# A third home for gathered expert rows, with the first tile's residual parked in DRAM and the score blocks placed anew

## The chip, the cores and the metric

The kernel runs on one core of a Trainium2 chip. The metric is device time in microseconds: 3100.5 us is the median of three executions before the change (3100.32, 3100.5 and 3105.6). The core has five engines, each with an instruction stream of its own that is run in order: TensorE (PE; its weight loads are listed as PEld), VectorE (DVE), ScalarE (ACT), GpSimd (POOL) and SyncE (SP), which only issues transfers. Transfers move through 16 DMA engines that all queues share.

## The reference, cut to what matters

```python
h = rms_norm(x); proj = h @ w_in                     # 512 tokens, width 2048
x = x + concat(rms_norm(attention), rms_norm(recurrent)) @ w_out
def peer_ffn(xn):                                    # 4 tiles of 128 tokens
    s1, s2 = scores of 2 x 128 keys, for 8 heads; top 16 of each, then of their sums
    e = i1 * 128 + i2                                # 128 experts per token, of 16384
    g = softmax(top)
    act = gelu(einsum('chkd,cd->chk', u_tab[e], xn))
    return einsum('chk,chkd->cd', g * act, v_tab[e])
x = x + peer_ffn(rms_norm(x))
```

## The kernel before

The attention and recurrent half fills about the first 640 us. After it, `acc` [128 x 4 x 2048] holds the residual of the four token tiles; it is also what the expert half adds to and what is written out. The normalised activations stand transposed in `FH` and `FL` (a high and a low part; every product is three matmuls, `mm3`).

**Two ways through the experts.** Tiles 1 to 3 (384 tokens) go through all 16384 experts as dense matmuls: 128 score blocks ("S": 128 experts x 384 tokens, 2 half blocks of 24 matmuls each), gelu, times a gate matrix, and then the value matmuls ("V"). Tile 0 is done by gathering: 128 rows of `u_tab` and then 128 of `v_tab`, 1 MB each (one row of 2048 floats for each of 128 tokens). `gather` issues one such transfer on GpSimd's queue; `side` is one side step: VectorE takes row j, forms a dot product with `xg` (j < 128) or adds it, weighted, into `acc[:, 0, :]` (j >= 128), and then calls `gather` for a later row. At j = 127 ScalarE's gelu and a product make the weights W0 from the dots.

**Weights stream.** `need` hands out the next half block in a fixed order and, first, issues the loads that come after (`emit_next`): a raw load of 512 KB on SP's queue, ScalarE's copy `hi` (L130), VectorE's remainder `lo` (L131). Four slots of hi and lo exist, so up to four half blocks are converted or being converted.

**The gate stage** (from about 965 us). `NB4` = 96 gate groups of four tokens build the gate matrix. For each, VectorE makes five one-hot products (`onehots`, L847, L848, L850; three buffers, two groups ahead), TensorE 12 small matmuls (L863), and ScalarE copies the result into the staging buffer `stg` (L865). There is one `stg`; it holds eight groups, then ScalarE's queue stores it to `GD` in DRAM (L868, 2 MB). Between the groups stand `park` calls: a score block whose gelu result is saved to DRAM (`AD`). 44 blocks are parked, ten before this stage, 32 in the loop (one for every third group) and two behind it. Side steps stand at groups 3, 9, ..., 39 and at every third group from 45: 24 in all, with one buffer for rows (`rowp`). In this part the order of the instructions on each engine is made by a scheduler from the program's order and its own estimate of when operands are ready.

**The main stage** (from about 1351 us) is written out in order by hand (`manual_schedule`). PSUM is divided anew (`ps_s`: two buffers pS; `ps_v`: six pV). The loop runs over `JOBS`: the S blocks 44 to 127, mixed with V jobs, then the V jobs of the parked blocks. `gates` loads a slice of GD on SP's queue. After each half unit `pace` adds 0.585 (0.43 for the parked part) to a debt, and each whole unit of it is one side step; rows have a second buffer in pool `ep`. What a job leaves behind (`fin`: gelu and gating, or the eviction of pV into `acc`, L996) is run in the next job. After the loop come the last evictions, the store of tiles 1 to 3, and any side steps that are left.

Of the kernel before, what the change touches and what calls it, by code (L numbers as in the profile page):

```python
# [7 lines left out]
F32 = mybir.dt.float32  # L8
# [8 lines left out]
DRAM = bass.MemoryType.DRAM  # L17

S, D = 512, 2048
# [18 lines left out]
def body(tc, nc, d, dbg=None):  # L38
    v, s, g, pe, sy = nc.vector, nc.scalar, nc.gpsimd, nc.tensor, nc.sync
# [3 lines left out]
    def pool(name, bufs=1, **kw):  # L43
        cm = tc.tile_pool(name=name, bufs=bufs, **kw)
        p = cm.__enter__()
        stk.append((p, cm))
        return p

    def close(p):
        i = [q is p for q, _ in stk].index(True)  # L50
        cm = stk.pop(i)[1]
        cm.__exit__(None, None, None)
# [4 lines left out]
    acc = accp.tile([128, NTT, D], F32, name="acc")  # L57
# [46 lines left out]
    pools = [base]  # L104
# [335 lines left out]
    for hb in range(2):  # L440
# [34 lines left out]
        for u in range(3):  # L475
            hi, lo = need("wuq", hb, u)
            for m in range(2):
# [5 lines left out]
                i = 2 * u + m  # L483
# [5 lines left out]
                else:  # L489
                    t_ = ap.tile([128, S], F32, name="qrx", bufs=3)  # L490
                    v.tensor_scalar(t_, ps, col(C_QHR), None, op0=OP.mult)
                    j = 2 * (i - 4)
# [115 lines left out]
    xg = xgp.tile([128, D], F32, name="xg")  # L608
# [23 lines left out]
    for k in range(KT):  # L632
        ps = bank()
        for t in range(NTT):
# [3 lines left out]
        v.scalar_tensor_tensor(XL[:, :, k, :], pv, col(C_FG + k), XH[:, :, k, :].bitcast(F32),  # L638
                               op0=OP.mult, op1=OP.subtract)
    v.tensor_tensor(xg, xns[0], grow, op=OP.mult)  # L640
    close(fp)
    egp = pool("eg", side="right")

# [3 lines left out]


    NCH = TD // 32
    dr = pool("dr", space=DRAM)  # L650
    GD = dr.tile([NCH, NBLK // GRP, 128, GRP * 32], F32, name="GD")
    AD = dr.tile([PARK, 128, TD], F32, name="AD")
    pkp = pool("park")
# [11 lines left out]
    def park():  # L665

        b = parked[0]
        if b >= PARK:
            return
        parked[0] += 1  # L670
        ps = bank()
        s_matmuls(b, ps[:, :TD])
        a = pkp.tile([128, TD], F32, name="pact", bufs=2)
        s.activation(a, ps[:, :TD], AF.Gelu)  # L674
        s.dma_start(AD[b], a)
# [123 lines left out]

    rowp = pool("rowp")  # L800
    rows, ng = {}, [0, 0]

    def gather(*pools):
        j = ng[0]
        if j >= 256:
            return
        ng[0] += 1
        r = pools[j % len(pools)].tile([128, D], F32, name="row", bufs=1)
        g.indirect_dma_start(out=r, out_offset=None, in_=d["un" if j < 128 else "vn"],  # L809
                             in_offset=bass.IndirectOffsetOnAxis(ap=E0[:, j % 128:j % 128 + 1], axis=0))  # L810
        rows[j] = r

    def side(*pools):

        j = ng[1]
        if j >= 256:
            return
        ng[1] += 1
        r = rows.pop(j)
        if j < 128:  # L820
            v.scalar_tensor_tensor(r, r, 1.0, xg, op0=OP.mult, op1=OP.mult, accum_out=dots[:, j:j + 1])  # L821
            if j == 127:
                s.activation(W0, dots, AF.Gelu)
                v.tensor_tensor(W0, W0, G0, op=OP.mult)
        else:
            v.scalar_tensor_tensor(acc[:, 0, :], r, W0[:, j - 128:j - 127], acc[:, 0, :], op0=OP.mult, op1=OP.add)  # L826
            if j == 255:
                g.dma_start(d["out"][0:128, :], acc[:, 0, :])
        gather(*pools)

    gp = pool("gate")
    iox = gp.tile([128, 64, 2], BF, name="iox")
    v.tensor_copy(iox, cst[:, K_IOTA:K_IOTA + 128].rearrange("p (a b) -> p a b", b=2))
    gather(rowp)
    NT = 4
    NB4 = TD // NT
    oh = {}

    def onehots(q):

        o2 = gp.tile([128, NT, 64, 2], BF, name="o2", bufs=3)
        o1 = gp.tile([128, NT, 64, 2], BF, name="o1", bufs=1)
        o3 = gp.tile([128, 3, NT, 64, 2], BF, name="o3", bufs=3)
        c = slice(NT * q, NT * q + NT)
        sh = [128, NT, 64, 2]
        io = iox[:, None].to_broadcast(sh)
        v.tensor_tensor(o2, io, e2T[:, c, None].to_broadcast(sh), op=OP.is_equal)  # L847
        v.tensor_tensor(o1, io, e1T[:, c, None].to_broadcast(sh), op=OP.is_equal)  # L848
        for j in range(3):
            v.tensor_tensor(o3[:, j], o1, g3T[:, j, c, None].to_broadcast(sh), op=OP.mult)  # L850
        oh[q] = (o2.rearrange("p t a b -> p t (a b)"), o3.rearrange("p j t a b -> p j t (a b)"))
# [3 lines left out]
    def gate_mm(q):  # L855

        o2, o1 = oh.pop(q)
        if q % 8 == 0:
            stg[0] = gp.tile([128, 128, 32], F32, name="stg", bufs=1)
        ps = bank()  # L860
        for i in range(4):
            for j in range(3):
                pe.matmul(ps[:, i * 128:(i + 1) * 128], o2[:, i], o1[:, j, i], start=j == 0, stop=j == 2)  # L863
        qq = q % 8
        s.activation(stg[0][:, :, qq * 4:(qq + 1) * 4].rearrange("p a t -> p t a"),  # L865
                     ps.rearrange("p (t a) -> p t a", t=4), AF.Copy)
        if qq == 7:
            s.dma_start(GD[q // 8].rearrange("g p x -> p g x"), stg[0].rearrange("p (g a) t -> p g (a t)", a=GRP))  # L868
# [1 line left out]
    for q in range(2):  # L870
        onehots(q)
    for q in range(NB4):
        if q % 3 == 0:
            park()
            if q % 6 == 3 or q > 42:
                side(rowp)
        if q + 2 < NB4:
            onehots(q + 2)
        gate_mm(q)
# [9 lines left out]
    ep = pool("ep")  # L889
# [31 lines left out]
    def pace(x):  # L921
        debt[0] += x
        while debt[0] >= 1:
            debt[0] -= 1
            side(rowp, ep)

    gather(rowp, ep)
    post = []
    def fetch(b):
        if b < PARK:  # L930
# [6 lines left out]
    for ji in range(PARK, len(JOBS)):  # L937
        job = JOBS[ji]
        if job[0] == "S":
# [4 lines left out]
            for hf in range(2):  # L944
                hi, lo = need("ud", b, hf)
                for k in range(8):
                    kk = hf * 8 + k
                    mm3(ps, hi[:, k * 128:(k + 1) * 128], lo[:, k * 128:(k + 1) * 128],
                        XH[:, 1:, kk, :], XL[:, 1:, kk, :], kk == 0, kk == KT - 1)
                if ji == PARK and hf == 0:  # L950
                    gates(b // GRP)
                for f in post:
                    f()
                post = []
                pace(RATE)
# [6 lines left out]
        else:  # L962
# [13 lines left out]
            for pr in range(2):  # L976
                hi, lo = need("vd", gi, dc, pr)
                for t in range(3):
                    for bj in range(2):
                        ph, pl = Pt[gi * GRP + 2 * pr + bj]  # L980
                        cs = slice(bj * 512, (bj + 1) * 512)
                        pe.matmul(pss[t], ph[:, t, :], hi[:, cs], start=pr + bj == 0, stop=False)  # L982
                        pe.matmul(pss[t], ph[:, t, :], lo[:, cs], start=False, stop=False)  # L983
                        pe.matmul(pss[t], pl[:, t, :], hi[:, cs], start=False, stop=pr + bj == 2)  # L984
                for f in post:
                    f()
                post = []
                if tail and pr == 1:
                    b = gn * GRP + dc
                    gated(At.pop(b), b)  # L990
                pace(0.43 if tail else RATE)
# [9 lines left out]
    for f in post:  # L1001
        f()
    while ng[1] < 256:
        side(rowp, ep)
    ctx.__exit__(None, None, None)
    while stk:
        close(stk[-1][0])
# [77 lines left out]
```

## Time and profile before

| | |
|---|---|
| median of three executions | 3100.5 us |
| profiled execution: own time, span of its instructions | 3107.04 us, 3104.9 us |
| PE busy | 3043.2 us, 98% |
| DVE, ACT, POOL busy | 74%, 35%, 13% |
| bytes moved | 691.13 MB, mean 223 GB/s |
| mean granted TensorE clock | 0.986 of full speed |
| main stage, 1360 to 3080 us | PE 1720.00 us busy, DMA engines 80% |

Times in the rows are from the start of the span. A row in brackets tells how long the engine stood idle before the instruction and what ended it. An engine name with a q (SPq) is its queue issuing a transfer.

### The profile page before, as it was taken

To read this page: it belongs to the slowest core of one execution; us is meant where nothing else is said; L and a number is where in the kernel's file an instruction comes from. 1 tells how busy PE (TensorE), PEld (TensorE's weight loads), DVE (VectorE), ACT (ScalarE), POOL (GpSimd) and SP (SyncE) were. 2 spreads that over 40 slices of the span, in tenths; PEclk is the share of its full clock that TensorE was granted. 3 is DMA by queue.
4 is the path that set the end of the run, shared out by engine and by line. 5 is a ranking of instruction groups with operands and counts; after the bars stand their busy time and mean duration, and the time that the engine had idled before them with its cause. 6 is when DMAs were issued, how large, how long until landed. Compare 5 with 4: busy or idle time off the path is not lost.

```text
span 3104.9 us, 39324 instructions
## 1 busy us (share of the span) xinstructions
PE 3043.2 (98%) x15443; PEld 2630.8 (85%) x15443; DVE 2284.7 (74%) x3456; ACT 1096.5 (35%) x1371; POOL 393.9 (13%) x280
## 2 busy tenths in 40 slices
PE   8999999999999999999999999999999999999999
PEld 7777565678899998999999999999999999888887
DVE  4465544448999888757777777777777777788887
ACT  4455332342234444443333333333333333333332
POOL 0000000000000011001212112122211212211111
PEclk9999898999999999999999999999999999999999
DMA  7222211232245887678787787877878778878876
GB/s 247 87 78 75 88 55 41 88 108 83 89 129 195 269 274 255 200 264 290 278 296 284 283 301 274 299 284 281 296 281 296 285 282 292 298 277 295 290 283 234
DMA packets 247306, 691.13 MB, mean 223 GB/s; under 512 B 17040, under 2 KB 128272, under 8 KB 213456
## 3 DMA queue, kind: packets, MB, share of 16 engines
q1 hardware_dynamic: 152832, 382.15, 36.8%
q0 software_dynamic: 37008, 269.50, 23.2%
q10 hardware_dynamic: 57280, 36.97, 3.9%
q8 instruction: 121, 1.98, 0.3%
q14 instruction: 65, 0.53, 0.0%
HBM read 650.40 MB, written 38.14 MB: 222 GB/s over the span
## 4 chain that ended last, share of the span: by engine, by line
PE 57%; issue 0%; DVE 0%; ACT 0%
PE pV L984 11%; PE pV L983 11%; PE pV L982 11%; PE pS L161 8%; PE pS L163 8%; PE pS L162 8%; PE ps L161 0%; PE ps L162 0%; PE ps L163 0%; PE ps L863 0%; DVE acc L996 0%; ACT pact L674 0%; DVE o L850 0%; ACT hi L130 0%
## 5 line engine op out<-in xcount | busy, mean ns | idle before, releaser
L130 ACT ACTIVATE hi<-raw 128x1024 fp32r<-128x1024 f32 x631 | 667.8, 1061 | 1489.4 <-PE pS L162 487.6
L131 DVE TENSOR_TENSOR lo<-raw,hi 128x1024 fp32r<-128x1024 f32 x631 | 771.1, 1222 | 495.2 <-ACT hi L130 481.6
L161 PE MATMUL pS<-FH,hi 128*128 128x384 f32 x1344 | 449.9, 335 | 1.3 <-ACT pact L674 1.3
L163 PE MATMUL pS<-FH,lo 128*128 128x384 f32 x1344 | 450.0, 335 | 0.0
L162 PE MATMUL pS<-FL,hi 128*128 128x384 f32 x1344 | 449.5, 334 | 0.0
L984 PE MATMUL pV<-hi,FL 128*128 128x512 f32 x960 | 374.7, 390 | 0.0
L983 PE MATMUL pV<-lo,FH 128*128 128x512 f32 x960 | 374.7, 390 | 0.0
L982 PE MATMUL pV<-hi,FH 128*128 128x512 f32 x960 | 373.4, 389 | 0.0
L161 PE MATMUL ps<-FH,hi 128*128 128x384 f32 (+1 forms) x960 | 342.8, 357 | 0.3 <-ACT hi L130 0.3
L809 POOL DMA_INDIRECT row<-in_un,E x128 | 175.6, 1372 | 1319.3 <-DVE row L821 819.3
L163 PE MATMUL ps<-FH,lo 128*128 128x384 f32 (+1 forms) x960 | 337.8, 352 | 0.6 <-DVE lo L131 0.6
L162 PE MATMUL ps<-FL,hi 128*128 128x384 f32 (+1 forms) x960 | 338.1, 352 | 0.0
L821 DVE SCALAR_TENSOR_TENSOR row<-row,xg 128x2048 f32<-128x2048 f32 x128 | 292.5, 2285 | 22.0 <-DMA row<-in_un,E 22.0
L826 DVE SCALAR_TENSOR_TENSOR acc<-row,W,acc 128x2048 f32<-128x2048 f32 x128 | 300.2, 2345 | 0.0
L809 POOL DMA_INDIRECT row<-in_vn,E x128 | 192.4, 1503 | 804.8 <-DVE acc L826 754.0
L161 PEld LDWEIGHTS pS<-FH,hi 128*128 128x128 f32 x1344 | 252.3, 188 | 4.7 <-ACT pact L674 1.7
L162 PEld LDWEIGHTS pS<-FL,hi 128*128 128x128 f32 x1344 | 252.3, 188 | 3.1
L163 PEld LDWEIGHTS pS<-FH,lo 128*128 128x128 f32 x1344 | 252.2, 188 | 0.0
L996 DVE TENSOR_TENSOR acc<-pV,acc 128x512 f32<-128x512 f32 x384 | 240.9, 682 | 8.3 <-PE pV L984 8.3
L984 PE MATMUL pV<-hi,pl 128*128 128x512 f32 x576 | 224.4, 390 | 0.0
L983 PE MATMUL pV<-lo,ph 128*128 128x512 f32 x576 | 224.2, 389 | 0.0
L982 PE MATMUL pV<-hi,ph 128*128 128x512 f32 x576 | 224.0, 389 | 0.0
(281 smaller groups left out, 4423.2 us busy)
## 6 DMA issues: line engine op xcount, KB each, us to landing
raw<-in_ud SPq DMA_DIRECT2D x256, 512.0 KB
raw<-in_vd SPq DMA_DIRECT2D x256, 512.0 KB
G<-GD SPq DMA_DIRECT2D x33, 768.0 KB
GD<-stg ACTq DMA_DIRECT2D x12, 2048.0 KB
raw<-in_win SPq DMA_DIRECT2D x44, 512.0 KB
raw<-in_wo SPq DMA_DIRECT2D x32, 512.0 KB
raw<-in_wq SPq DMA_DIRECT2D x32, 512.0 KB
AD<-pact ACTq DMA_DIRECT2D x44, 192.0 KB
```

The costliest lines, as they stand in the source:

```text
L130: s.activation(hi, raw, AF.Copy)
L131: v.tensor_tensor(lo, raw, hi.bitcast(F32), op=OP.subtract)
L161: pe.matmul(out, ah, bh, start=start, stop=False)
L162: pe.matmul(out, ah, bl, start=False, stop=False)
L163: pe.matmul(out, al, bh, start=False, stop=stop)
L809: g.indirect_dma_start(out=r, out_offset=None, in_=d["un" if j < 128 else "vn"], in_offset=bass.IndirectOffsetOnAxis(ap=E0[:, j % 128:j % ...
L821: v.scalar_tensor_tensor(r, r, 1.0, xg, op0=OP.mult, op1=OP.mult, accum_out=dots[:, j:j + 1])
L826: v.scalar_tensor_tensor(acc[:, 0, :], r, W0[:, j - 128:j - 127], acc[:, 0, :], op0=OP.mult, op1=OP.add)
L982: pe.matmul(pss[t], ph[:, t, :], hi[:, cs], start=pr + bj == 0, stop=False)
L983: pe.matmul(pss[t], ph[:, t, :], lo[:, cs], start=False, stop=False)
L984: pe.matmul(pss[t], pl[:, t, :], hi[:, cs], start=False, stop=pr + bj == 2)
L996: v.tensor_tensor(a, pss[t], a, op=OP.add)
```

## The change

Tile 0's residual, `acc[:, 0, :]`, is stored to a DRAM buffer `RD` before the gate stage, on SP's queue. From then until side step 127 this part of `acc` is a home for gathered rows; after step 127 GpSimd's queue loads the residual back, and from there `xg`, whose last reader was step 127, is a home instead. A table, `row_buf`, says where row j goes: two homes in the gate stage (the first 19 rows), three in the main stage. `side` now issues gathers until it is `ahead` of the steps by two, or three in the main stage; the first 19 gathers belong to the gate stage.

Blocks stand at groups 0, 3 and 6 of every eight groups, until 44 are parked; side steps stand at group 0 of every eight and at group 11 of every sixteen: 18 in all. `RATE` and the other paces are as before.

```diff
+    dr = pool("dr", space=DRAM)
+    RD = dr.tile([128, D], F32, name="RD")
+    sy.dma_start(RD, acc[:, 0, :])
     close(fp)
...
+    NG0 = 19
+    late = {}
+    def row_buf(j):
+        if j < NG0:
+            i = j % 2
+        else:
+            i = (j - NG0 + NG0 % 2) % 3
+        if i == 0:
+            return rowp.tile([128, D], F32, name="row", bufs=1)
+        if i == 1:
+            return acc[:, 0, :] if j < 128 else xg
+        return late["ep"].tile([128, D], F32, name="row", bufs=1)
-    def gather(*pools):
+    def gather():
...
-        r = pools[j % len(pools)].tile([128, D], F32, name="row", bufs=1)
+        r = row_buf(j)
...
                 v.tensor_tensor(W0, W0, G0, op=OP.mult)
+                g.dma_start(acc[:, 0, :], RD)
...
-        gather(*pools)
+        if j + ahead[0] >= NG0 and "ep" not in late:
+            return
+        while ng[0] < min(256, ng[1] + ahead[0]):
+            gather()
+    ahead = [2]
...
-    gather(rowp)
+    gather()
+    gather()
...
-        if q % 3 == 0:
+        if q % 8 in (0, 3, 6):
             park()
-            if q % 6 == 3 or q > 42:
-                side(rowp)
+        if q % 8 == 0 or q % 16 == 11:
+            side()
...
-            side(rowp, ep)
-    gather(rowp, ep)
+            side()
+    late["ep"] = ep
+    ahead[0] = 3
+    while ng[0] < ng[1] + 3:
+        gather()
...
     while ng[1] < 256:
-        side(rowp, ep)
+        side()
```

## Rows read from the trace of the kernel before

**Rows 1.** The page: TensorE's busy time, share of the span and instructions.
```profile
PE 3043.2 (98%) x15443; PEld 2630.8 (85%) x15443; DVE 2284.7 (74%) x3456; ACT 1096.5 (35%) x1371; POOL 393.9 (13%) x280
```

**Rows 2.** Windows: length, busy PE, PEld, DVE, ACT, POOL; clock, DMA share, GB/s.
```profile
970.64:987.23 16.59, 12.30 (x85) 11.41 (x85) 14.35 (x28) 5.42 (x6) 1.89 (x2) 0.90 0.61 214
987.23:1255.51 268.28, 249.84 (x1934) 244.05 (x1933) 222.35 (x436) 122.56 (x138) 27.48 (x22) 0.96 0.80 265
...
1160.42:1170.83 10.41, 10.41 (x86) 10.25 (x85) 9.49 (x19) 5.56 (x6) 1.68 (x1) 1.00 0.75 257
1255.51:1328.36 72.85, 72.85 (x590) 71.75 (x589) 49.14 (x112) 35.70 (x41) 0.00 (x0) 1.00 0.57 174
1328.36:1350.85 22.49, 19.36 (x134) 18.66 (x133) 9.00 (x11) 11.12 (x14) 1.08 (x1) 1.00 0.75 219
1360.00:3080.00 1720.00, 1720.00 (x8503) 1540.41 (x8502) 1364.84 (x1382) 538.57 (x630) 336.15 (x230) 1.00 0.80 287
```

**Rows 3.** Timeline of ScalarE, end of the gate stage and first blocks after it.
```profile
1334.51 0.38 ACTq L868 DMA_DIRECT2D GD<-stg  x1
...
1345.20 1.06 ACT L130 ACTIVATE hi<-raw 128x1024 fp32r<-128x1024 f32 x1 [2.72 <-PE ps L162]
1349.36 1.06 ACT L130 ACTIVATE hi<-raw 128x1024 fp32r<-128x1024 f32 x1 [3.10 <-PE ps L162]
...
1359.97 1.06 ACT L130 ACTIVATE hi<-raw 128x1024 fp32r<-128x1024 f32 x1 [3.76 <-DMA raw<-in_ud]
```

**Rows 4.** Waits, 970 to 1351 us: waiter and releaser, total, times, longest.
```profile
ACT stg L865 <- DMA GD<-stg: 61.7, 11, 11.0
DVE lo L131 <- ACT hi L130: 38.4, 12, 7.1
...
DVE row L821 <- DMA row<-in_un,E: 19.9, 13, 3.8
PE ps L863 <- ACT stg L865: 12.3, 3, 5.3
PE ps L863 <- DVE o L850: 11.4, 4, 4.3
```

**Rows 5.** Timeline of ScalarE around two stores of stg (groups 31 and 39).
```profile
1093.25 0.38 ACTq L868 DMA_DIRECT2D GD<-stg  x1
...
1104.12 1.14 ACT L865 ACTIVATE stg<-ps 128x512 f32<-128x512 f32 x1 [2.83 <-DMA GD<-stg]
...
1123.62 0.38 ACTq L868 DMA_DIRECT2D GD<-stg  x1
...
1139.43 2.10 ACT L865 ACTIVATE stg<-ps 128x512 f32<-128x512 f32 x2 [10.97 <-DMA GD<-stg]
```

**Rows 6.** Tiles row and out: transfers from issue to landing, us.
```profile
DMA to landing us min/median/max: 5.4/7.3/10.7
...
DMA to landing us min/median/max: 4.4/4.4/4.4
```

**Rows 7.** Timelines of VectorE and GpSimd, the last 23 us.
```profile
3082.82 2.35 DVE L826 SCALAR_TENSOR_TENSOR acc<-row,W,acc 128x2048 f32<-128x2048 f32 x1
...
3099.82 0.69 DVE L996 TENSOR_TENSOR acc<-pV,acc 128x512 f32<-128x512 f32 x1 [0.67 <-PE pV L984]
...
3085.46 0.58 POOL L828 DMA_DIRECT2D out<-acc  x1 [9.13 <-DVE acc L826]
```

**Rows 8.** Timeline of VectorE in the gate stage; line 821, 970 to 1351 us.
```profile
1133.29 1.22 DVE L131 TENSOR_TENSOR lo<-raw,hi 128x1024 fp32r<-128x1024 f32 x1
...
1136.10 0.42 DVE L848 TENSOR_TENSOR o<-iox,e1T 128x512 bf16<-128x512 bf16 x1
...
1136.77 1.09 DVE L850 TENSOR_TENSOR o<-o,g3T 128x512 bf16<-128x512 bf16 x3
...
L821 DVE SCALAR_TENSOR_TENSOR row<-row,xg x24: 2279/2291/2293, 973.0 to 1234.4; 128x2048 f32<-128x2048 f32 x24
```

**Rows 9.** Timeline of SP's queue after the gate stage's last store.
```profile
1346.40 0.38 SPq L895 DMA_DIRECT2D G<-GD  x1
```

More of the change, by code (lines that the diff above doesn't have):

```diff
@@ L649, in body @@
     NCH = TD // 32
-    dr = pool("dr", space=DRAM)
     GD = dr.tile([NCH, NBLK // GRP, 128, GRP * 32], F32, name="GD")
@@ L811, in gather, with side @@
         rows[j] = r
-    def side(*pools):
+    def side():
         j = ng[1]
```

## The prediction, made before the kernel ran

> **What bounds the kernel now.** I read the page first: TensorE is busy 98% of the span [rows 1], so only TensorE's lost time, or work behind its last matmul, can move the end. Then I cut the span into windows at the starts of gate groups [rows 2]. From 1360 to 3080 us TensorE is busy for all 1720.00 us at full clock: nothing that VectorE, the gathers or the loads do there costs time now, and nothing can be won there. The loss to look at is in the gate stage.
>
> A clean period of that stage, one score block and three gate groups, takes 10.41 us (third window of [rows 2]). A half block takes 4.16 us, read from the two ScalarE splits that start as its slots come free, at 1345.20 and 1349.36 [rows 3]; a block is so 8.32 us and a gate group (10.41 - 8.32) / 3 = 0.70 us. Against that price the windows lose:
> - start, 970.64 to 987.23: 16.59 - 10.41 = 6.2 us, at a clock of 0.90;
> - middle, 987.23 to 1255.51, 23 periods: 268.28 - 23 x 10.41 = 28.9 us, at 0.96;
> - 1255.51 to 1328.36, 7 periods: 72.85 - 72.87 = 0;
> - end, 1328.36 to 1350.85, three gate groups and the two blocks that trail the loop: 22.49 - 2.1 - 16.6 = 3.8 us.
> That is 38.9 us. The views of waits say whom TensorE waited for: gate matmuls for the copies into stg (12.3 us) and for one-hots (11.4 us) [rows 4]; the rest is matmuls at the lower of the two clock levels (1.2 of 2.4 GHz) after such a gap. Behind both stands the single stg: ScalarE waits 61.7 us, 11 times, for the store of the previous 32 columns, and while it stands its splits stand too, so VectorE's lo waits for hi (38.4 us) and one-hots queue behind it [rows 4]. A store takes 10.9 us when a block follows it soon (issued 1093.25, next copy 1104.12) and 15.8 us at its longest (1123.62 to 1139.43) [rows 5]. The last seven periods have the same kind of waits, but no side step, and lose nothing: it takes stg's wait and VectorE's side steps together.
>
> **The change part by part.** *Saving RD.* One 1 MB store on SP's queue before the stage, whose source is long ready. It lies under projections; a direct 1 MB transfer landed after 4.4 us [rows 6]. I take 0, with 4.4 as upper bound if the loads queued behind it were late.
>
> *Homes of rows.* Two in the stage, three afterwards. VectorE waited 19.9 us for rows in the stage [rows 4], which can go. After 1360 us TensorE has no gap to give back: 0. Side steps are 2.35 us each [rows 7]; there are still 256.
>
> *Side steps in the stage: 18 instead of 24.* The order on the engines is the scheduler's, and it runs them as early as it can, about one in every period: all 24 of them start between 973.0 and 1234.4 us, though the program has the last at group 93 [rows 8]. This is why the 7 periods have none. VectorE's own work in a period is 3 x 1.69 us of one-hots (0.67 from the start of an o1 to that of the three o3, an o2 between, and 1.02 for these) and two lo of 1.22 us [rows 8], 7.5 of 10.41 us. One side step fits, and a third more now that two rows can wait. So I expect 18 steps packed into the first half, at the density of before or above.
>
> *Blocks at groups 0, 3 and 6 of eight.* Each reuse of stg now has a block, 8.32 us, between the store and the copy that waits for it. With a store of 10.9 us ScalarE's wait falls to 2 to 4 us, with 15.8 to at most 8. I take the middle loss from 28.9 to 8 us: two or three us at each of the first three or four reuses, where side steps are dense, nothing later, as in the quiet window. Bounds: 0 (as that window) and 20 (two thirds of today's, if side steps decide). The start I leave at 6.2, since the first step still waits for its row ahead of a one-hot; bounds 5 and 10.
>
> *The end of the stage.* Blocks come 3 to every 8 groups, so the 34 that are left are used up at group 88: seven gate groups and then the switch of PSUM pools have no block beside them. Call t the end of that last block. The store of groups 80 to 87 is issued two copies after group 87, about 6.2 us before t (8.3 for the block, less 2.1), and lands after 10.9 us, at t + 4.7; then eight copies of 1.05 us [rows 5] follow, done at t + 13.1. One-hots cannot be sooner than t + 10: five groups wait for a buffer and take 1.69 us each. The last store is issued at t + 13. Before, it was issued at 1334.51 and 1346.40 is when SP could go on to the gate load that waits for it, 11.9 us [rows 3, 9]; the two trailing blocks covered that. SP's queue holds the raw loads for block 46 on behind that gate load. From 1346.40 to the split of raw half 46:1, which waited for its load, was 13.6 us (1359.97) [rows 3, 9], and right behind that split (1.06) on ScalarE stands the first gelu of pS (0.5); block 46 needs the PSUM buffer that it frees. So block 46 can start 11.9 + 15.2 = 27 us after the last store's issue, at t + 40. Without any loss it would start at t + 5.6 (eight gate groups) + 16.6 (blocks 44 and 45) = t + 22.2. The loss is 18 us, and some 2 us of lower clock behind the gap: 20 us, against 3.8 now, so +16. Bounds: +5 (if a hit at the raw loads is smaller because only 46:0 matters and the burst lands in half the time) and +21 (a store of 15.8 us there).
>
> *The tail.* I counted the paced steps: 424 half units with 0.585 or 0.43 each make 234. Before, 24 + 234 is more than 256 and the last step ran at 3082.82, 17 us ahead of the last eviction (3099.82) [rows 7]. Now 18 + 234 = 252: four steps follow the last eviction, in the written order. From the end of that eviction: step 252, 2.35 us; it frees the home of row 255, whose gather lands 5.4 to 10.7 us after its issue [rows 6], about 6 with little else moving: 2.35 + 0.25 + 6 = 8.6, later than steps 253 and 254 (7.05); step 255 ends at 11.0; the store of out is issued 0.3 us later (3085.17 to 3085.46 [rows 7]) and lands in 4.4. Before, the final store took the same 4.4 us from the same eviction. So +11 us, bounds 10 (5.4) and 16 (10.7). The Trainium skill (DMA: Bandwidth & Descriptors, Anatomy of one DMA) gives 2.0 us plus bytes over 436 GB/s for a transfer issued from GpSimd, an estimated 4.4 us for this 1 MB row; by it the tail would be +9.4 instead of +11. The rows show no gather under 5.4 us, so the measured value stands.
>
> *Restoring RD.* The load is issued by GpSimd behind side step 127, and step 128 now comes one half unit (4.15 us) later. It will stand some 4 us for the landing, and lo and evictions behind it. TensorE has two split half units in hand, 8.3 us: 0, bound +4.
>
> **Sum.** Start 0, middle -20.9, end +16, tail +11, RD 0: +6 us. The profiled execution took 3107.04 us for a span of 3104.9, above the median of 3100.5; the difference is set on the median: 3106.5 us. A change of 0.2%, 6.2 us, is about what these runs can tell from none.
>
> **The rivals.** *A, the forecast* (+6, own range -3 to +14), 0.45; of it 0.29 inside 0.2% and 0.16 above.
>
> *B, side steps fill VectorE and the middle stalls stay.* For it: all the loss lies where side steps are, and they stay at least as dense. Against: the first reuses that follow a block at once have short stores. Middle 20 instead of 8: +18, 3118.5 us. It decides if more than half of the first five reuses still hold a gate matmul over 3 us. 0.20, slower.
>
> *C, the end is covered.* If the last store lands while blocks 44 and 45 still run and raw half 46:1 is in time, the end costs +5 and not +16; with the middle at 3 the sum is -25.9 + 5 + 11 = -10, 3090.5 us. For it: slots held four halves before, 16.6 us of work. Against: the load came 13.6 us after SP was free. It decides if block 46 starts within 3 us of block 45's end. The Trainium skill (Trainium Kernel Development and Optimization, Best Practices) advises double buffering, and by that rule the second home alone should pay; the rows give it 11.4 us of one-hot waits at most, -11.4 without the end and the tail. 0.22: 0.19 faster, 0.03 the same.
>
> *D, the middle has less to give outside the profile.* The profiled run is 6.5 us longer than the median; if these are stg stalls, the middle gives 14.4 and the sum is +12.5, 3113 us. Nothing in the rows speaks against it. 0.13, slower.
>
> Together: faster 0.19, within 0.2% 0.32, slower 0.49. Range: C's 3090.5 at the low end, B's 3118.5 with two us of the tail's bound at the high end: 3090 to 3120.
>
> **What would show it.** The stage's window in the new trace: gate matmuls waiting after group 48 should be gone, but a gap before the gate groups 91 to 95, before the first pS and before block 46, with SP's gate load late. After the last pV eviction four side steps, the last of them waiting for its row. I am wrong if block 46 is not late, if the middle keeps its gaps, or if steps 252 to 255 run ahead of the last eviction.

## The result, and the profile after

The changed kernel takes 3137.74 us (median of four, 3136.38 to 3142.51) against 3103.05 us of the kernel before beside it (median of four, 3100.32 to 3113.49): ratio 1.0108, 95% interval 1.0081 to 1.0135. It is slower by about 35 us, outside the predicted range, whose upper end was 3120. The profiled execution has a span of 3134.5 us against 3104.9, and these 29.6 us are what the traces can place.

The page of the changed kernel first: TensorE's busy time is the same to 0.4 us [rows 1], so what was added is time in which it stood idle.

```profile
PE 3043.6 (97%) x15443; PEld 2630.3 (84%) x15443; DVE 2284.6 (73%) x3456; ACT 1096.4 (35%) x1371; POOL 397.0 (13%) x281
```

The windows of the changed kernel, cut as in [rows 2] at gate groups: groups 0 to 2 with a block, groups 3 to 23, groups 24 to 87, groups 88 to the first block of the main stage, from there to block 46, and from there to the last matmul's end.

```profile
966.74:988.27 21.53, 14.65 (x86) 13.07 (x85) 18.48 (x32) 5.66 (x6) 2.81 (x3) 0.76 0.81 284
988.27:1098.32 110.05, 85.57 (x637) 82.48 (x637) 85.01 (x153) 39.69 (x45) 16.93 (x14) 0.91 0.73 254
1098.32:1342.75 244.43, 244.43 (x1922) 240.66 (x1921) 169.18 (x369) 121.60 (x136) 0.00 (x0) 1.00 0.64 198
1342.75:1355.67 12.92, 8.64 (x97) 6.68 (x96) 9.55 (x25) 9.15 (x10) 0.00 (x0) 0.81 0.21 61
1355.67:1379.14 23.47, 19.35 (x97) 19.03 (x97) 3.84 (x4) 2.50 (x3) 1.87 (x2) 0.86 0.92 292
1379.14:3114.07 1734.93, 1734.93 (x8544) 1551.57 (x8544) 1379.73 (x1401) 538.10 (x630) 342.07 (x234) 1.00 0.81 288
```

With the prediction's prices, 8.32 us a block and 0.70 us a group, the first window loses 11.1 us; the second, 21 groups and 8 blocks, 110.05 - 81.3 = 28.8; the third, 64 groups and 24 blocks, 244.43 - 244.5 = 0; the fourth, 8 groups, 7.3; the fifth, two blocks, 6.8. The last window is 2.7 us longer than in the kernel before (1732.2 by the same cut): from 1379.14 to 1395.70 us the mean granted clock was 0.83, behind the start of block 46 in the kernel before 1.00, and 0.17 of 16.6 us is an estimated 2.8 us. The difference of the spans:

| part | before | after | difference | predicted |
|---|---|---|---|---|
| begin of the first gate group | 970.6 | 966.7 | -3.9 | 0 |
| start (groups 0 to 2) | 6.2 | 11.1 | +4.9 | 0 |
| middle (groups 3 to 87) | 28.5 | 28.7 | +0.2 | -20.9 |
| end, up to block 46 and behind it (7.3 + 6.8 + 2.7) | 3.8 | 16.8 | +13.0 | +16 |
| start of the last matmul to end of span | 5.5 | 20.8 | +15.3 | +11 |
| sum | | | +29.5 | +6 |

(Before, the middle lost 28.9 in the prediction's windows, which ended at group 72 and then lost nothing; cut at group 88 it is 28.5.)

The waits of the changed kernel between 966 and 1356 us. They answer to [rows 4]:

```profile
ACT stg L887 <- DMA GD<-stg: 71.8, 11, 15.3
DVE lo L131 <- ACT hi L130: 57.9, 18, 11.6
...
PE ps L885 <- DVE o L872: 33.3, 10, 12.1
...
DVE row L837 <- DMA row<-in_un,E: 4.5, 4, 1.4
```

The second home did what it was for: VectorE's wait for rows in `row` fell from 19.9 to 4.5 us. But ScalarE's wait for stg rose from 61.7 to 71.8 us, although each copy that reuses stg now has a block ahead of it. The stores themselves are longer. ScalarE's timeline at the first store and at the fifth:

```profile
1002.35 0.38 ACTq L890 DMA_DIRECT2D GD<-stg  x1
...
1025.47 2.73 ACT L887 ACTIVATE stg<-ps 128x512 f32<-128x512 f32 x3 [15.28 <-DMA GD<-stg]
...
1153.21 0.40 ACTq L890 DMA_DIRECT2D GD<-stg  x1
...
1165.10 3.01 ACT L887 ACTIVATE stg<-ps 128x512 f32<-128x512 f32 x3 [4.04 <-DMA GD<-stg]
```

From issue to the next copy the first store takes 23.1 us and the fifth 11.9; before it was 10.9 to 15.8 [rows 5]. The second took 22.5, the third 18.1, the fourth 14.3; the fifth to the tenth take 11.5 to 12.6 and the eleventh 8.8.

What else used the 16 DMA engines meanwhile is in the view of the queues (packets, MB, share of the 16 engines): q0 carries GpSimd's gathers, q10 ScalarE's stores, q1 SP's loads. First store (1002.35 to 1025.47 us), fifth (1153.21 to 1165.10) and last (1355.65 to 1364.46):

```profile
q0 software_dynamic: 576, 4.19, 46.5%
q10 hardware_dynamic: 4398, 2.49, 34.6%
q1 hardware_dynamic: 483, 1.72, 18.2%
...
q10 hardware_dynamic: 4317, 2.37, 64.7%
q1 hardware_dynamic: 311, 1.14, 35.6%
...
q10 hardware_dynamic: 4112, 2.10, 84.9%
```

In the first two of these windows q10 also carries the results of parked blocks, 0.3 to 0.4 MB. The store's queue has 34.6% of 23.1 us, 64.7% of 11.9 and 84.9% of 8.8, which is 8.0, 7.7 and 7.5 us, so the store's own work is nearly the same in all three. The rest of the first store's time went to gathers (10.8 us) and raw loads (4.2 us), and the packets of the three queues together fill 99% of the engines' time. No more than two gathers are in flight at once, but 4.19 MB is four of them: side steps go on while the store is under way, and each frees a home for the next gather. The fourth store has no gather beside it any more, but 2.1 MB of raw loads. And the two stores of [rows 5] were not alone either; q0 in their windows (1093.25 to 1104.12 and 1123.62 to 1139.43 us of the kernel before):

```profile
q0 software_dynamic: 95, 0.65, 17.7%
...
q0 software_dynamic: 286, 2.09, 40.0%
```

Line 837, the side step, shows what goes on meanwhile (counts, min/median/max ns, first and last start):

```profile
L837 DVE SCALAR_TENSOR_TENSOR acc<-acc,xg x9: 2277/2283/2293, 959.1 to 1093.8; 128x2048 f32<-128x2048 f32 x9
...
L837 DVE SCALAR_TENSOR_TENSOR row<-row,xg x9: 2282/2286/2293, 973.1 to 1087.0; 128x2048 f32<-128x2048 f32 x9
```

The 18 steps, spread over 96 groups in the program, run between 959.1 and 1093.8 us, one per 7.9 us (before: 24 in 261 us, one per 11 [rows 8]), and with them their gathers. How a long store reaches TensorE is seen on VectorE's timeline ahead of the gap of 11.8 us in front of group 13 (gaps are given from the start of one matmul to the start of the next):

```profile
1029.09 1.23 DVE L131 TENSOR_TENSOR lo<-raw,hi 128x1024 fp32r<-128x1024 f32 x1 [8.30 <-ACT hi L130]
...
1030.57 2.29 DVE L837 SCALAR_TENSOR_TENSOR row<-row,xg 128x2048 f32<-128x2048 f32 x1
...
1032.78 1.14 DVE L872 TENSOR_TENSOR o<-o,g3T 128x512 bf16<-128x512 bf16 x3
```

VectorE stands 8.30 us at a lo whose hi is behind ScalarE's standing copy, then does the lo and a side step that the order has put ahead, and only then the one-hots for which TensorE waits.

The end of the stage came as predicted. ScalarE's timeline, then SP's queue [rows 3, 9]:

```profile
1355.65 0.38 ACTq L890 DMA_DIRECT2D GD<-stg  x1
...
1377.65 1.06 ACT L130 ACTIVATE hi<-raw 128x1024 fp32r<-128x1024 f32 x1 [5.38 <-DMA raw<-in_ud]
1378.61 0.47 ACT L984 ACTIVATE pact<-pS 128x384 f32<-128x384 f32 x1
```

```profile
1364.46 0.38 SPq L917 DMA_DIRECT2D G<-GD  x1
```

The last store is issued at 1355.65 and landed after 8.7 us with nothing beside it (11.9 was taken); the gate load, free from then, is followed by the raw loads; the second of them lets its split begin 13.2 us later (13.6 was taken), and block 46 starts behind the gelu, at 1379.14.

The tail, VectorE and then GpSimd [rows 7], and the transfer's time from the list of issues:

```profile
3114.11 0.69 DVE L1021 TENSOR_TENSOR acc<-pV,acc 128x512 f32<-128x512 f32 x1 [0.67 <-PE pV L1009]
...
3124.91 2.35 DVE L843 SCALAR_TENSOR_TENSOR acc<-row,W,acc 128x2048 f32<-128x2048 f32 x1 [3.08 <-DMA row<-in_vn,E]
```

```profile
3117.33 2.93 POOL L825 DMA_INDIRECT row<-in_vn,E  x1 [7.22 <-DVE acc L843]
3127.56 0.58 POOL L845 DMA_DIRECT2D out<-acc  x1 [7.31 <-DVE acc L843]
```

```profile
out<-acc POOLq DMA_DIRECT2D x1, 1024.0 KB, 4.2
```

Four steps follow the last eviction, from 3114.72 us on; the last waits for row 255, 7.6 us after its gather began (6 was taken), and the span ends 6.9 us after the store's issue (4.4 was taken).

### The profile page after: what moved, and what is told of

It is laid out like the page before. It is cut to its first block, busy times and chain, and to the rows that moved or that the text cites. A ratio compares the mean times of both kernels' runs of the same rounds, so it can differ in the third digit from the quotient of the medians.

```text
span 3134.5 us, 39313 instructions
## 1 busy us (share of the span) xinstructions
PE 3043.6 (97%) x15443; PEld 2630.3 (84%) x15443; DVE 2284.6 (73%) x3456; ACT 1096.4 (35%) x1371; POOL 397.0 (13%) x281
## 4 chain that ended last, share of the span: by engine, by line
PE 90%; DVE 5%; DMA 2%; ACT 1%; issue 1%; SPq 0%; POOL 0%; POOLq 0%; ACTq 0%; DVEq 0%
PE pV L1008 11%; PE pV L1009 11%; PE pV L1007 11%; PE ps L161 7%; PE ps L163 7%; PE ps L162 7%; PE pS L161 7%; PE pS L163 7%; PE pS L162 7%; PE ps L388 2%; PE ps L389 2%; PE ps L387 2%; DMA GD<-stg 2%; PE ps L885 2%; PE ps L546 1%
## 5 line engine op out<-in xcount | busy, mean ns | idle before, releaser
L1009 PEld LDWEIGHTS pV<-hi,FL 128*128 128x128 f32 x960 | 180.1, 188 | 37.8
L1007 PEld LDWEIGHTS pV<-hi,FH 128*128 128x128 f32 x960 | 180.2, 188 | 35.3
L1008 PEld LDWEIGHTS pV<-lo,FH 128*128 128x128 f32 x960 | 180.2, 188 | 35.4
L825 POOL DMA_INDIRECT row<-in_un,E x82 | 111.6, 1362 | 753.4 <-DVE row L837 477.7
## 6 DMA issues: line engine op xcount, KB each, us to landing
GD<-stg ACTq DMA_DIRECT2D x12, 2048.0 KB, 11.9
```

## The experiments

Two theories of the middle at first. T (transfers): the gathers stretch stg's store. V (VectorE): the packed side steps fill VectorE. For each kernel the loss of the middle is that of groups 3 to 87, with the prices above; the number of blocks in it differs, so the working is given. All kernels below but the two without steps were executed once. The kernel with another pace, whose gate stage is that of the changed kernel, loses 28.5 us in the middle (354.21 - 325.7) where that one loses 28.7.

**Small gathers.**

```diff
+    row0 = rowp.tile([128, D], F32, name="row0")
+    v.memset(row0, 0.0)
...
         if i == 0:
+            return row0
...
+        n = 16 if j < NG0 else 128
-        g.indirect_dma_start(out=r, ...
-                             in_offset=...(ap=E0[:, j % 128:j % 128 + 1], axis=0))
+        g.indirect_dma_start(out=r[:n], ...
+                             in_offset=...(ap=E0[:n, j % 128:j % 128 + 1], axis=0))
```

> The first 19 gathers move 16 partitions of a row tile instead of 128 (128 KB instead of 1 MB each; the other partitions hold old data, so the output differs); the side steps on VectorE are as in the changed kernel, and as dense or denser. Theory T (transfers): two homes let gathers bunch, and these stretch the store of stg from 11 us (as after group 40 in the changed kernel) to 23, 22, 18 and 14 us; ScalarE, then lo, then one-hots stand for it. T expects the first four stores at 10 to 13 us and the gaps of 11.8 and 12.3 us at groups 12 and 20 gone (under 2 us), the span about 25 us under the changed kernel's 3134.5. Theory V (VectorE): the packed side steps fill VectorE and delay the one-hots; V expects the gaps to stay (8 us or more each) although the stores are short.

Measured: span 3115.1. The middle's window:

```profile
992.75:1324.10 331.35, 328.28 (x2557) 322.07 (x2557) 254.25 (x521) 162.57 (x181) 15.93 (x14) 0.99 0.64 194
```

85 groups and 32 blocks are 325.7 us, so it loses 5.6 us instead of 28.7; the largest gap is 2.3 us. The span fell by 19 us and not by 25. The first store, in ScalarE's timeline:

```profile
1006.79 0.38 ACTq L895 DMA_DIRECT2D GD<-stg  x1
1018.95 3.03 ACT L892 ACTIVATE stg<-ps 128x512 f32<-128x512 f32 x3 [4.27 <-DMA GD<-stg]
```

12.2 us instead of 23.1. The 18 steps were as dense, 963 to 1076 us. T holds, V alone does not.

**Quick steps.**

```diff
+            w = 512 if j < 18 else D
-            v.scalar_tensor_tensor(r, r, 1.0, xg, ...
+            v.scalar_tensor_tensor(r[:, :w], r[:, :w], 1.0, xg[:, :w], ...
```

> The first 18 side steps work on 512 of the 2048 columns of a row (the dots of these rows are partial, so the output differs), about 0.7 us instead of 2.3 us of VectorE each; gathers are whole. T expects stores of 18 us and more again and at least one gap over 8 us between groups 8 and 24. V expects gaps under 3 us and the stage about 25 us shorter, whatever the stores take.

Measured: span 3125.6; the first two stores as long as in the changed kernel (23.1 and 22.3 us on ScalarE's timeline; the first):

```profile
1002.66 0.41 ACTq L891 DMA_DIRECT2D GD<-stg  x1
1025.78 2.73 ACT L888 ACTIVATE stg<-ps 128x512 f32<-128x512 f32 x3 [15.26 <-DMA GD<-stg]
```

The middle, 988.74 to 1332.94 us, loses 18.5 us (344.2 - 325.7). After the first store TensorE has two gaps close together, of 4.1 and 6.0 us; after the second only 1.6 and 1.7. T's wording (a gap of over 8 us) fails by its letter, V's (under 3) too. Shorter steps give back 10 of 28.7 us: VectorE's load decides in part what a long store costs.

**One home.**

```diff
-            i = j % 2
+            i = 0
-    ahead = [2]
+    ahead = [1]
-    gather()
     gather()
```

> One home for rows in the gate stage (one gather in flight), all else as in the changed kernel: 18 side steps, blocks at groups 0, 3 and 6 of eight, four steps left for the tail. T expects stores of 11 to 16 us as before the change, no gap over 4 us after group 8, and the middle of the stage at a loss of 3 to 10 us instead of 29: a span of about 3112 us. A rival, that the new place of the blocks itself does the harm, expects the gaps of 11 to 12 us to stay, 3130 us or more. V, whose steps are now one a period again, expects 5 to 12 us less.

Measured: span 3141.2. T was wrong here: the middle loses 31.0 us (356.78 - 325.7), with gaps of 2.6 to 4.1 us at each of the first five reuses. The middle's window, then the first store on ScalarE's timeline:

```profile
991.31:1348.09 356.78, 338.73 (x2558) 331.39 (x2557) 259.64 (x522) 160.69 (x181) 17.43 (x16) 0.96 0.70 221
...
1005.21 0.42 ACTq L889 DMA_DIRECT2D GD<-stg  x1
1021.83 2.77 ACT L886 ACTIVATE stg<-ps 128x512 f32<-128x512 f32 x3 [8.74 <-DMA GD<-stg]
```

With one gather in flight at a time the store still takes 16.6 us, later ones without steps 11.6 to 13.0. Two homes make the loss come in two large pieces, one home in five; the sum is nearly the same. What this left open, whether the gather or the blocks' new place does it, the last two kernels settle.

**Blocks at their old place.**

```diff
-        if q % 8 in (0, 3, 6):
+        if q % 3 == 0:
             park()
```

> Blocks at every third group again, so that two blocks trail the loop; two homes, 18 side steps and the tail as in the changed kernel. T expects stores of 18 us and more in the first third of the stage and at least as much loss in the middle as now (29 to 45 us); the end of the stage, from the last gate group to the start of block 46, back to a loss of some 4 us from 17. If the place of the blocks is the cause, the middle falls to 25 us or less.

Measured: span 3133.5. The middle loses 40.3 us (332.74 less 85 groups and 28 blocks, 292.5), ScalarE waits up to 15.4 us for a store; the end loses 2.3 us and block 46 starts 16.8 us after the first block, as before the change. So the new place takes 12 us off the middle when gathers are dense, and gives 14 back at the end (7.3 + 6.8 against 2.3 and 0.1, and 2.7 behind it).

**The pace.**

```diff
-    RATE = 0.585
+    RATE = 0.605
```

> The changed kernel with the pace 0.605 instead of 0.585, so that 18 + 241 paced steps are more than 256 and none is left behind the last eviction. If the four left steps make the tail, the time from the last matmul to the end falls from 20.8 us to the 5.5 us of the kernel before, and the span from 3134.5 to about 3119; nothing else moves. Rival: VectorE's extra steps or the store of out on GpSimd's queue still stretch the tail; then it stays above 10 us.

Measured: span 3117.5, tail 6.3 us, main stage from block 46 on 1734.4 us, TensorE busy throughout. VectorE's last instruction is again an eviction, and no step stands behind it:

```profile
3111.66 0.69 DVE L1021 TENSOR_TENSOR acc<-pV,acc 128x512 f32<-128x512 f32 x1 [0.67 <-PE pV L1009]
```

The tail of 20.8 us falls to 6.3, so the four steps left over are 14.5 of the 15.3 us by which the tail had grown, and the main stage has room for them.

**Two blocks behind the loop.**

```diff
-        if q % 8 in (0, 3, 6):
+        if q % 8 in (0, 3, 6) and parked[0] < PARK - 2:
```

> The changed kernel with the last two blocks taken out of the loop, so that they trail it as before the change. If the missing cover makes the loss at the end, block 46 starts 16.6 us after the first block of the main stage (23.5 now), and the last eight groups lose under 4 us; the loop's last third has fewer blocks to cover groups, which may cost a few us there. Span about 3122. Rival: the loss comes from something else at the switch, and block 46 stays late by 5 us or more.

Measured: span 3131.0. Windows of groups 3 to 87, 88 to the main stage, and blocks 44 and 45:

```profile
986.23:1329.02 342.79, 315.57 (x2461) 308.11 (x2461) 246.37 (x507) 157.48 (x177) 16.09 (x14) 0.96 0.68 217
1329.02:1361.62 32.60, 30.02 (x192) 25.80 (x192) 16.80 (x40) 12.42 (x14) 0.94 (x1) 0.79 0.69 202
1361.62:1378.37 16.75, 16.75 (x97) 16.75 (x97) 9.55 (x9) 4.09 (x5) 0.94 (x1) 1.00 0.93 329
```

Block 46 is on time (16.75 us), so the missing cover was its cause. But with the two blocks taken from the loop twelve groups stand bare instead of seven: the middle loses 33.7 (342.79 - 309.1 for 30 blocks) and the last eight groups with the two blocks 10.4 us. The expectation of 4 us, and of 3122 for the span, was wrong: cover was moved, not made.

**The kernel before without steps in the stage.**

```diff
-            if q % 6 == 3 or q > 42:
-                side(rowp)
-    RATE = 0.585
+    RATE = 0.66
```

> The kernel before, with no side step in the gate stage and the pace 0.66 instead of 0.585, so that all 256 are in the main stage. Theory T and V both: no gathers and no steps there, so the middle of the stage loses under 4 us instead of 28.5, and the main stage, where TensorE has no gap now, takes 24 more steps (56 us of VectorE in 1750) for nothing: a span of 3070 to 3078 us against 3104.9, ratio 0.990. Rival: the main stage's VectorE and DMA are nearer to full than the rows show, and the steps that come there cost as much as they cost in the stage: ratio 0.997 or more.

Measured: 3072.29 us (median of four) against 3108.32 of the kernel before beside it (seven), ratio 0.988, interval 0.9863 to 0.9896; span 3071.0. It beats both kernels. Windows: groups 3 to 87, 88 to the main stage, block 46 to the last matmul:

```profile
980.58:1276.55 295.97, 293.57 (x2366) 288.01 (x2365) 213.25 (x476) 150.22 (x169) 0.00 (x0) 1.00 0.62 190
1276.55:1316.91 40.36, 39.02 (x291) 38.38 (x288) 20.10 (x38) 19.30 (x23) 0.94 (x1) 1.00 0.73 229
...
1333.66:3065.80 1732.14, 1732.14 (x8545) 1548.87 (x8544) 1422.20 (x1437) 538.00 (x628) 386.63 (x254) 1.00 0.83 300
```

The start loses 0.7 us (11.08 - 10.4), the middle 3.5 (with 28 blocks), the end 1.5; the main stage takes the 24 steps with TensorE busy all the time, VectorE at 82% and the DMA engines at 83%.

**The changed kernel without steps in the stage.**

```diff
-        if j < NG0:
-            i = j % 2
-        else:
-            i = (j - NG0 + NG0 % 2) % 3
+        i = j % 3
-    NG0 = 19
+    NG0 = 2
-        if q % 8 in (0, 3, 6):
+        if q % 8 in (0, 3, 6) and parked[0] < PARK - 2:
             park()
-        if q % 8 == 0 or q % 16 == 11:
-            side()
-    RATE = 0.585
+    RATE = 0.66
```

> The changed kernel with no side step in the gate stage, the pace 0.66, three homes in the main stage from the first row on, and two blocks behind the loop. If homes and the blocks' place are worth nothing where there is no gap, it equals the kernel before without steps, within 0.2%. If the blocks around the reuse of stg or the third home help, it is faster than that one by 5 us or more.

Measured: 3080.44 us, ratio to the kernel before 0.9911 (0.9894 to 0.9927), span 3077.0: slower than the last one, not equal. Groups 88 to the main stage:

```profile
1289.28:1322.19 32.91, 30.25 (x193) 26.10 (x193) 16.80 (x40) 12.42 (x14) 0.94 (x1) 0.79 0.67 195
```

The middle, with 30 blocks, loses 3.4 us (312.55 - 309.1), as without the new place; the end 10.7, its bare groups. The third home changes nothing in a main stage that has no gap (1731.8 us from block 46 to the last matmul's start in both).

**Small stores.**

```diff
+    for c in range(NCH):
+        g.dma_start(GD[c].rearrange(...), d["un"][c * 256:(c + 1) * 256].rearrange(...))
...
-            s.dma_start(GD[q // 8].rearrange(...), stg[0].rearrange(...))
+            s.dma_start(GD[q // 8, :, :16].rearrange(...), stg[0][:16].rearrange(...))
```

> The changed kernel, homes, steps, blocks and whole gathers as they are, but each store of stg moves 16 of the 128 partitions (the rest of the gate buffer in DRAM is filled with other data by DRAM-to-DRAM copies before the gate stage, so the output differs and the stretch before the stage may be some us longer). If the way from gathers to the gaps leads through stg's store and ScalarE's wait for it, ScalarE waits under 1 us per reuse, and the middle of the stage loses under 6 us instead of 28.7 although gathers and steps are as dense. If gathers or steps hurt in another way (late raw loads, VectorE full), 15 us or more stay.

Measured: the stage begins 21 us later, so the span, 3128.1, says little; the middle loses 6.9 us (332.64 - 325.7). ScalarE's wait for stores, 960 to 1350 us:

```profile
ACT stg L889 <- DMA GD<-stg: 1.8, 2, 1.0
```

Gathers whole, steps as dense (980 to 1094 us), store short: some 22 of 28.7 us are gone, though the loss is not quite under the 6 us expected. The way from gathers to TensorE leads through stg's store. The rest, 6.9 us here and 5.6 with small gathers, is what packed steps cost without a long store.

**One home, small gathers.** The edits of the third and the first experiment together.

> One home in the stage as before (18 steps, one gather in flight), with gathers of 16 partitions (other rows of data, output differs). With whole gathers the stores took 16.6 us and the middle lost 31.0 us. If a single gather in flight already stretches the store, the first stores take 11 to 12 us here and the middle loses under 6 us. If the blocks' place or the steps cause that loss, 15 us or more stay.

Measured: span 3104.9. The middle's window and the first store on ScalarE's timeline:

```profile
986.21:1312.98 326.77, 326.41 (x2557) 320.83 (x2556) 258.92 (x522) 162.63 (x181) 17.89 (x16) 1.00 0.65 195
```

```profile
1000.12 0.41 ACTq L894 DMA_DIRECT2D GD<-stg  x1
1012.75 3.04 ACT L891 ACTIVATE stg<-ps 128x512 f32<-128x512 f32 x3 [4.76 <-DMA GD<-stg]
```

The loss is 1.0 us instead of 31.0, the store 12.6 us instead of 16.6. So whole gathers, one at a time, were the cause; the blocks' place was not, and neither were the steps, which come one per 10.3 us here.

## Why the prediction was wrong

**The step that failed** is "Blocks at groups 0, 3 and 6 of eight": "With a store of 10.9 us ScalarE's wait falls to 2 to 4 us, with 15.8 to at most 8. I take the middle loss from 28.9 to 8 us". It took the store's duration from two rows as if it were the store's own. It is what the gathers beside it leave: 12 us with small gathers, 16.6 with whole ones one at a time, 23 with two in flight (four in all while the store lasts). The two rows themselves, 10.9 and 15.8 us, had 0.65 and 2.09 MB of gathers beside them. The step on the homes counted the waits that a second home saves, and put what its transfers take from others at nothing; the step on the side steps had already said that these, and so their gathers, would be packed as densely or more, and the two were not put together. The middle kept its loss, 28.7 us after 28.5. That is 21 of the 23.5 us between the sum of +6 and the measured +29.5.

**Rival B** was nearer, with the stalls to stay, but it priced the middle at 20 us against the measured 28.7, and its reason holds only in part. VectorE's load decides how fast a delay is caught up (quick steps: 18.5 us left), but without the long store the packed steps cost 6 to 7 us (small store, small gathers). Its test, more than half of the first five reuses with a gap over 3 us, failed too: two of five had one, each over 11 us.

**The start** was off by 4.9 us: with two rows at hand, three side steps were put ahead of the one-hots of group 2, and without steps the start loses 0.7. That the stage began 3.9 us earlier was not foreseen, and no run here shows why.

**The end** was right as a mechanism: bare groups, late last store, SP's queue standing with the gate load, the split and the gelu behind the second raw load. It was 3 us too dear, because the last store landed after 8.7 and not 11.9 us; its 2 us of lower clock are the 2.7 us behind the start of block 46.

**The tail** was right as a mechanism, and under-sized by 4 us: 1.6 at the last gather (7.6 for 6) and 2.5 at the end, of which the landing explains none (4.2 us); the 2.7 us from landing to the end of the span stay unexplained. The estimate by the formula of the Trainium skill (DMA: Bandwidth & Descriptors, Anatomy of one DMA), +9.4, was further off than the row's.

**The restore of RD and the third home** were right: VectorE stood 3.5 us for RD, and TensorE was busy for the whole of the last window.

**Rivals C and D** fell: the end was not covered, and the medians are further apart (34.7 us) than the profiled spans (29.6), where D had them closer.

**How the gathers get ahead of the store** can be read from the packets. Between 1015.2 and 1017.4 us, within the first store of the changed kernel (packets, MB, share of the 16 engines):

```profile
q0 software_dynamic: 103, 0.83, 90.5%
q10 hardware_dynamic: 110, 0.06, 8.4%
```

The gathers and the store moved about as many packets, but a packet is 8 KB for a gather and 0.5 KB for the store. The Trainium skill (DMA: Bandwidth & Descriptors, Queues, rings and completion order) says that a DMA engine takes turns between queues packet by packet. The trace agrees, with 103 packets against 110. That a store with larger packets would be held up less is argued, not shown; no run here changed the packets.

## What to carry to other kernels

Before more room is given to transfers, look where what they share the engines with is waited for: here gathers of 1 MB, up to two in flight and four in all, lengthened a 2 MB store from 12 to 23 us, and an in-order engine that waited for the store carried it to TensorE. Work with slack belongs where the bound engine has no gaps and its helpers have room, even if that place is already the busier one: moving all side steps out of the gate stage gave 1.2%, and no arrangement inside it that was run here came near that. When steps are moved between two paced places, count them to the end: a pace left at 0.585 put four steps, 14.5 us, behind the last eviction.

## What the runs showed of the hardware that was not expected

The same 2 MB store took 8.7 us with nothing beside it, 11.5 to 14.3 us with raw loads, 16.6 us with whole gathers one at a time and 22 to 23 us with two in flight, while its own queue had the 16 engines for 7.5 to 8.0 us in the three stores looked at. So a store's time from issue to landing tells little of its own cost: it is that of all that the engines move meanwhile.

A stretch where TensorE starves costs more than its gaps, and here several short gaps added more than two long ones. The window of 110.05 us with two gaps of about 12 us had a mean granted clock of 0.91 (two levels, 1.2 and 2.4 GHz), so that of its 28.8 us of loss about 4.3 lie outside the 24.5 us in which TensorE was not busy. With one home the middle, with five gaps of 2.6 to 4.1 us, had a clock of 0.96 over 356.78 us: TensorE was not busy for 18.1 us, and 13.0 of the 31.0 us of loss lie outside.
